# Streaming output projection in another chunk order, an indexer without GpSimd, and a solve and an input that come in pieces

## The chip, the cores and the metric

The kernel runs on one core of a Trainium2 chip. The metric is the device time of one execution in microseconds (us). The engines are TensorE (PE in the rows, with its weight loads as PEld), VectorE (DVE), ScalarE (ACT), GpSimd (POOL) and SyncE (SP, which here only issues DMAs); 16 DMA engines serve the core's queues.

## What is computed

One layer of an encoder block on x of 256 tokens by 2048 channels, in fp32. One input projection feeds two groups of heads: sparse attention (8 heads x 128, with an indexer that keeps each query's 64 highest-scored admissible keys) and RWKV-7 time mixing (16 heads x 64). Their outputs, side by side, go through one output projection; then comes a mixture of 16 experts.

```python
h = rms_norm(x, g_mix)
proj = h @ w_in
y_dsa = dsa_mixer(...)             # indexer scores, top-k, softmax attention
y_rwkv = rwkv7_mixer(...)          # token shift, delta-rule scan, group norm, gate
x = x + concat(y_dsa, y_rwkv) @ w_out
h = rms_norm(x, g_ffn)
# hier_moe: 1 of 4 groups, 2 of its 4 experts per token, SwiGLU experts
x = x + hier_moe(h, ...)
```

## The kernel before

**Weights stream.** Both projections are matmuls in which each fp32 weight is used as the sum of two fp32r parts, and so is the input (three products each). `drive()` walks one long list, `stream`, of chunks of 128 partitions x 512 columns of weights: SP loads two at a time (512 KB) into three raw places (`RA` lower and upper half, `RB`), up to 8 chunks ahead; ACT copies a chunk to its high part (line 205), DVE subtracts it from the raw chunk to get the low part (line 206), into four slots `W`; PE then runs that chunk's matmuls (`pp`). `add_cm` chunks belong to RWKV's input blocks (12 matmuls of 256 columns), `add_tm` chunks to attention's columns and to the output projection (6 matmuls of 512 columns: 3 products for each of 2 token halves). A column chunk c0 to c3 of the output projection is 512 output columns and 16 chunks of the stream, one for each 128 channels of the mixed output: r0 to r7 from the RWKV blocks, h0 to h7 from the attention heads. `YSLOTS` gives their order in each column chunk, and a chunk needs the event that its `y` is there. Two banks `pp` hold a column chunk's sums, of four.

**What sets the order.** PE's order is written out by a planner, `Order`, that keeps its own time: generators (chains) yield a number (come back so much later) or a name (come back after that event), and between two chunks of the stream `drive()` lets every chain run that is ready. The chains are `rwkv_early(b)`, `solve(b)` and `rwkv_late(b)` for the 8 RWKV blocks (128 channels each), `kidx`, `qidx`, `qk`, `indexer` and `attention` for the sparse attention, `spread` for the input's norm, and `u_chain(cc)` behind each column chunk. The other engines' order is made by a scheduler from the program's order and the waits.

**RWKV blocks.** `rwkv_early(b)` ends with small matrices written to DRAM (`din`). `solve(b)` is on POOL: it reads `din` back, each partition its own copy (`at`, 512 KB in one DMA, line 650), then does 31 steps of a triangular solve on `xt` (two tensor_tensor each, lines 655 and 657; step s reads column s of `at`), and sends the result out and back (`dout`, `XT`: lines 658 and 660). `rwkv_late(b)` starts on PE with the matmul `pz<-R,XT`, then `pz<-z,A`, `pq`, `pc`, `pS`, `py`, `ptp`, `pv`, and gives chunk `r{b}` (`yT`).

**Attention.** `indexer()` builds scores `acc` on DVE query block by query block; a POOL memset masks a corner of it (line 872), then 8 rounds of `max` and `match_replace` on DVE find the top 64. Each head's `yps` and `ptp` matmuls give h0 to h7.

**The input's norm.** x (2 MB) is loaded in one DMA (`xt_`) behind the first weights; ACT squares it in four pieces with sums, `rstd` follows, and `spread()` makes `rsB` (1/rms for all tokens on every partition) by one matmul `rps` after a fixed 16.1 us. The first use of `rsB` is `shift()`, which frees a block's `pp` bank; DSA's columns use `rstd`.

**Behind the mixers.** When c0 is summed, `u_done(0)` calls `enter_moe()`: it asks for the event "rw closed" (the last `rwkv_late` is over) and all y, sets up the MoE's tiles, and POOL loads x again by column chunk (`load_x(cc)`, to `uu`; x(0) there, the others from within the output projection, line 1168, each behind a POOL copy that waits for the newest `W`). `u_chain(cc)` adds the sums to `uu`, transposes it (`utp`, 8 matmuls, copied to `uT`) and makes the router's logits `pl`; c(n) needs `u(n-1)` before its own `u_chain`.

**Expert weights.** 192 chunks of 1 MB go through a ring of 20 places, some of which are the space of `hT`, `W`, `RA` and others that must first be free. The first three are loaded after the last `rwkv_early`; `leave_rwkv` loads the next after the last `rwkv_late`, `prefetch_step` then one for every 2.2 weight loads, and at step c = 3 of c3 a burst fills the ring up to `n_early` = 15 chunks (line 1171), with one more each at c = 3, 7, 11 and 15. All are SP DMAs, in SP's order with the loads of `wo`. The experts' phase then runs pair after pair.

Of the kernel before, what the change touches and what calls it, by code (L numbers as in the profile page):

```python
# [17 lines left out]
P = 128  # L18
T = 256
D = 2048  # L20
# [7 lines left out]
CLAMP = -80.0  # L28

CON = [("cent", P), ("mask_s", 64), ("mask_bd", P), ("mask21", 64), ("scanm", T), ("xt0", 128), ("mu", 27), ("vecs", 64)]  # L30
YSLOTS = ["r0", "r1", "r2", "r3", "r4", "r5", "h0", "h1", "h2", "h3", "r6", "r7", "h4", "h5", "h6", "h7"]
EB1, EB2, EB = 9, 4, 20
FIRST = 1
WARM = 19
# [82 lines left out]
def block_kernel(ctx: ExitStack, tc: tile.TileContext, a: dict, dbg=None):  # L117
# [121 lines left out]
    with tc.tile_pool(name="xload", bufs=1) as xp:  # L239
        gT = xp.tile([P, KT], F32, name="gT")  # L240
        SP.dma_start(out=gT, in_=a["gT"])
        xT = [xp.tile([P, 4, T], F32, name=f"xT{q}") for q in range(4)]
        xt_ = xp.tile([P, 2, D], F32, name="xt_")

        def load_xT(q, r0, r1):
            SP.dma_start(out=xT[q][:, r0:r1, :], in_=a["xT"][:, 4 * q + r0:4 * q + r1, :])

        def load_w(n):
            c = (0, 1, 0)[n] * 1024
            return load_raw(a["wr"][(1, 1, 0)[n], :, c:c + 1024], 2 if n == 0 else 1)  # L250

        load_xT(0, 0, 2)
        raw0 = load_w(0)
        load_xT(0, 2, 4)
        load_xT(1, 0, 4)
        raw1 = load_w(1)
        load_xT(2, 0, 4)
        load_xT(3, 0, 4)
        first[0].update(zip((4, 5), load_w(2)))
        SP.dma_start(out=ident, in_=a["ident"])  # L260
        SP.dma_start(out=xt_, in_=a["x"].rearrange("(j p) m -> p j m", p=P))
        for q in range(4):
            for r in range(4):
                if q == 0 and r == 1:
                    first[1].update({k: split(raw0[k]) for k in range(2)})
                if q == 1 and r == 2:
                    first[1].update({2 + k: split(raw1[k]) for k in range(2)})
                g = gT[:, 4 * q + r:4 * q + r + 1]
                hi = hT[q][:, 0, r, :]
                ACT.activation(out=hi, in_=xT[q][:, r, :], func=AF.Copy, scale=g)  # L270
                DVE.scalar_tensor_tensor(out=hT[q][:, 1, r, :], in0=xT[q][:, r, :], scalar=g, in1=hi.bitcast(F32), op0=ALU.mult, op1=ALU.subtract)
        sq = xp.tile([P, D // 2], F32, name="sq")
        part = xp.tile([P, 2, 2], F32, name="part")
        for j in range(2):
            for c in range(2):
                ACT.activation(out=sq, in_=xt_[:, j, c * (D // 2):(c + 1) * (D // 2)], func=AF.Square, accum_out=part[:, j, c:c + 1])
        DVE.tensor_tensor(out=rstd, in0=part[:, :, 0], in1=part[:, :, 1], op=ALU.add)
        ACT.activation(out=rstd, in_=rstd, func=AF.Ln, scale=1.0 / D, bias=eps6)
        ACT.activation(out=rstd, in_=rstd, func=AF.Exp, scale=-0.5)

    def spread():

        yield RSTD_US
        ps = pbank("rps")
        dg = temp("kd")
        for j in range(2):
            DVE.tensor_scalar(dg[:, j * P:(j + 1) * P], ident, rstd[:, j:j + 1], None, ALU.mult)
        mm(ps[:, 0:T], ones, dg)
        ACT.copy(out=rsB, in_=ps[:, 0:T])
        od.event("rsB", Y[22])  # L290
# [29 lines left out]
    def tables():  # L320
        cs128 = att.tile([P, 2, 2, 64], F32, name="cs128", tag="qr", bufs=2)
        gq = att.tile([P, 2, 128], F32, name="gq", tag="qo", bufs=2)
        SP.dma_start(out=cs128, in_=a["cs128"])
        SP.dma_start(out=cs64, in_=a["cs64"])
        SP.dma_start(out=gq[:, 0, :], in_=a["q_gain"].broadcast_to([P, 128]))
        SP.dma_start(out=gq[:, 1, :], in_=a["k_gain"].broadcast_to([P, 128]))
        for s in range(2):
            for j in range(2):
                for hf in range(2):
                    g1 = gq[:, s, hf * 64:(hf + 1) * 64]  # L330
                    go = gq[:, s, (1 - hf) * 64:(2 - hf) * 64]
                    POOL.tensor_tensor(out=cg[:, s, j, hf * 64:(hf + 1) * 64], in0=cs128[:, j, 0, :], in1=g1, op=ALU.mult)
                    POOL.tensor_tensor(out=sg_[:, s, j, hf * 64:(hf + 1) * 64], in0=cs128[:, j, 1, :], in1=go, op=ALU.mult)
                POOL.tensor_scalar(sg_[:, s, j, 0:64], sg_[:, s, j, 0:64], -1.0, None, ALU.mult)
        POOL.tensor_scalar(sn64[:, :, 0, :], cs64[:, :, 1, :], -1.0, None, ALU.mult)
        POOL.tensor_copy(sn64[:, :, 1, :], cs64[:, :, 1, :])
# [189 lines left out]
    def rwkv_early(b):  # L526
# [15 lines left out]
        cs = temp("e1")  # L542
        DVE.tensor_tensor_scan(cs, scanm, sa[:, 0, :], 0.0, ALU.mult, ALU.add)
        Dt = temp("Dt", 2)[:, 0:260].rearrange("p (c t) -> p c t", c=4)
        POOL.memset(Dt[:, :, 0:1], 1.0)
        ACT.activation(out=Dt[:, :, 1:65], in_=cs.rearrange("p (c t) -> p c t", c=4), func=AF.Exp, scale=-C0)
        di = temp("di")
        ACT.activation(out=di, in_=cs, func=AF.Exp, scale=C0)
# [95 lines left out]

    def solve(b):

        at = tmp.tile([P, 32, 32], F32, name="at", bufs=1)
        xt = tmp.tile([P, 4, 32], F32, name="xt", bufs=1)
        tt = tmp.tile([P, 128], F32, name="tt", bufs=1)
        SQ.dma_start(out=at, in_=dr[b][0].rearrange("(o ci) u s t -> o (ci u) (s t)", o=1).broadcast_to([8, 16, 1024]))  # L650
        POOL.tensor_copy(xt, xt0)
        for s_ in range(31):
            n, m = s_ // 8 + 1, 31 - s_
            tv = tt[:, 0:n * m].rearrange("p (u t) -> p u t", u=n)
            POOL.tensor_tensor(out=tv, in0=xt[:, 0:n, s_:s_ + 1].broadcast_to([P, n, m]),  # L655
                               in1=at[:, s_:s_ + 1, s_ + 1:32].broadcast_to([P, n, m]), op=ALU.mult)
            POOL.tensor_tensor(out=xt[:, 0:n, s_ + 1:32], in0=xt[:, 0:n, s_ + 1:32], in1=tv, op=ALU.subtract)  # L657
        SQ.dma_start(out=dr[b][1].rearrange("ci w (i q) t -> q (ci w) i t", q=8), in_=xt.rearrange("p i t -> p (i t)"))
        for ci in range(4):
# [187 lines left out]
    def indexer():  # L847
# [3 lines left out]
        for j in range(2):  # L851
# [3 lines left out]
            for q in range(4):  # L855
# [13 lines left out]
                        else:  # L869
                            DVE.scalar_tensor_tensor(out=acc[:, :nk], in0=rl[:, b2, :nk], scalar=wx[:, j, hd:hd + 1], in1=acc[:, :nk], op0=ALU.mult, op1=ALU.add)  # L870
                yield 2 * Y[17]
            POOL.memset(acc[0:64, nk - 64:nk], NEG)
            for _ in range(8):
                m8 = att.tile([P, 8], F32, name="m8", bufs=2)
                DVE.max(m8, acc[:, :nk])
# [137 lines left out]
    def enter_moe():  # L1013
# [20 lines left out]
        xv = a["x"].rearrange("(j p) m -> p j m", p=P)  # L1034
        mo_["xv"] = xv
        load_x(0)
        for n in ("wrt", "gF", "iota", "utri", "rsum"):
            POOL.dma_start(out=mo_[n], in_=a[n])
        POOL.tensor_tensor(out=mo_["wrt"], in0=mo_["wrt"], in1=mo_["gF"].rearrange("p (k o) -> p k o", o=1).broadcast_to([P, KT, 32]), op=ALU.mult)
# [126 lines left out]

    def wo_after(cc):
        def after(c):
            if c == 4 and cc:
                load_x(cc)  # L1170
            if c % 4 == 3 and cc == 3:
                while len(ring) < n_early:
                    load_chunk(len(ring), True)
                load_chunk(len(ring) + 1)
        return after

    for cc in range(4):
# [354 lines left out]
```

## Times and profile before

| | |
|---|---|
| median of 3 runs | 1102.25 us (1102.21 to 1104.61) |
| the profiled execution | 1108.09 us |
| its span, first to last instruction | 1106.1 us |
| PE busy | 1034.8 us (94%) |
| DVE, ACT, POOL busy | 535.7, 384.0, 258.6 us |
| mean granted TensorE clock | 0.973 |
| moved by DMA | 298.74 MB, mean 270 GB/s |

The profile is one execution. Its span leaves 1.99 us of that execution's 1108.09 us to what lies around it. In the rows, an idle time in brackets stands before the first of a group of instructions on that engine, with what released it. A granted clock of 0.50 is the lower of TensorE's two levels, 1.2 of 2.4 GHz.

### The profile page before, as it was taken

What the parts mean: (1) busy time and instruction counts of PE and PEld (TensorE: products, weight loads), DVE (VectorE), ACT (ScalarE), POOL (GpSimd) and SP (SyncE); (2) the same over time, 40 slices, a digit from 0 to 9 for tenths busy, and PEclk for the clock granted to TensorE, in tenths of its full rate; (3) what the DMA queues carried; (4) which work ended last, traced back from release to release, by engine and by line L of the source; (5) the groups of instructions that cost most, each with busy time, mean ns of one, the idle gap of its engine ahead of it and who ended that gap; (6) DMA issues with size and microseconds to landing.
All of it is one profiled execution on the core that took longest, in us unless ns stands there. A gap on an engine that the chain in (4) does not pass through costs nothing.

```text
span 1106.1 us, 17189 instructions
## 1 busy us (share of the span) xinstructions
PE 1034.8 (94%) x6466; PEld 698.7 (63%) x6466; DVE 535.7 (48%) x1193; ACT 384.0 (35%) x816; POOL 258.6 (23%) x666
## 2 busy tenths in 40 slices
PE   5999999989899999898799789999999999999996
PEld 5999888967698877686577654444444343434342
DVE  5887668777768776855354231313121313121212
ACT  6666555646446564644244211000000101010101
POOL 1416572648346535353110100000000000000000
PEclk9999999999999998998799899999999999999998
DMA  8566554454345543445299969999999999999995
GB/s 317 166 187 191 162 153 150 124 140 127 118 141 181 161 143 101 141 124 207 72 331 330 394 252 364 364 420 420 420 421 421 420 420 419 421 420 420 420 417 202
DMA packets 62266, 298.74 MB, mean 270 GB/s; under 512 B 9040, under 2 KB 12928, under 8 KB 37856
## 3 DMA queue, kind: packets, MB, share of 16 engines
q1 hardware_dynamic: 56720, 289.29, 69.6%
q0 software_dynamic: 5456, 8.28, 3.1%
q8 instruction: 53, 0.87, 0.3%
q14 instruction: 37, 0.30, 0.1%
HBM read 294.37 MB, written 3.15 MB: 269 GB/s over the span
## 4 chain that ended last, share of the span: by engine, by line
PE 77%; DMA 7%; DVE 5%; ACT 4%; POOL 3%; issue 2%; SPq 1%; ACTq 0%; DVEq 0%; POOLq 0%
PE pp L130 27%; PE pd L130 10%; PE gate L130 10%; PE up L130 10%; PE misc L130 6%; DMA RA<-wo 4%; PE sc L130 3%; PE pz L130 2%; DVE W L206 2%; PE py L130 2%; DMA xt__114<-x 1%; POOL xt L657 1%; ACT W L205 1%; POOL tt L655 1%; PE pc L130 1%
## 5 line engine op out<-in xcount | busy, mean ns | idle before, releaser
L130 PE MATMUL pp<-W,hT 128*128 128x512 f32 x768 | 194.3, 405 | 6.5 <-DVE W L206 6.5
L206 DVE TENSOR_TENSOR W<-RA,W 128x512 fp32r<-128x512 f32 x200 | 137.5, 697 | 98.9 <-ACT W L205 97.0
L130 PE MATMUL pp<-hT,W 128*128 128x256 f32 x1296 | 174.0, 292 | 11.8 <-ACT W L205 10.5
L130 PEld LDWEIGHTS pp<-hT,W 128*128 128x128 f32 x1296 | 164.5, 197 | 15.7 <-ACT W L205 10.7
L205 ACT CAST W<-RA 128x512 fp32r<-128x512 f32 x200 | 122.1, 619 | 133.5 <-PE pp L130 87.6
L130 PEld LDWEIGHTS pp<-W,hT 128*128 128x128 f32 x768 | 144.4, 193 | 38.0 <-DVE W L206 7.4
L130 PE MATMUL pp<-W,yT 128*128 128x512 f32 x384 | 99.5, 414 | 13.7 <-ACT yT L890 6.6
L655 POOL TENSOR_TENSOR tt<-xt,at 128x24 f32<-128x24 f32 (+23 forms) x248 | 89.6, 361 | 72.8 <-DMA at<-din 54.1
L130 PEld LDWEIGHTS pp<-W,yT 128*128 128x128 f32 x384 | 74.4, 198 | 34.0 <-ACT W L205 8.0
L657 POOL TENSOR_TENSOR xt<-xt,tt 128x24 f32<-128x24 f32 (+23 forms) x248 | 89.1, 359 | 19.3
L206 DVE TENSOR_TENSOR W<-RB,W 128x512 fp32r<-128x512 f32 x100 | 68.7, 695 | 38.8 <-ACT W L205 38.3
L130 PE MATMUL pd<-ew,R 128*64 128x512 f32 x352 | 81.1, 598 | 2.7 <-ACT R L1376 2.7
L205 ACT CAST W<-RB 128x512 fp32r<-128x512 f32 x100 | 61.0, 619 | 60.4 <-PE pp L130 45.5
L130 PE MATMUL up<-ew,R 128*64 128x512 f32 x352 | 79.3, 592 | 0.0
L130 PEld LDWEIGHTS misc<-sel,uu 128*128 128x128 f32 x512 | 59.6, 192 | 15.2 <-issue 13.8
L1386 ACT ACTIVATE Y<-pd,sv 128x512 fp32r<-128x512 f32 x32 | 22.0, 688 | 126.8 <-PE pd L130 126.8
L1387 DVE SCALAR_TENSOR_TENSOR Y<-pd,sv,Y 128x512 fp32r<-128x512 f32 x32 | 24.0, 751 | 83.0 <-ACT Y L1386 83.0
L130 PE MATMUL misc<-sel,uu 128*128 128x128 f32 x512 | 63.0, 278 | 0.7 <-DVE sel L1308 0.7
L1396 DVE TENSOR_TENSOR x<-x,sc 128x512 f32<-128x512 f32 x56 | 36.0, 685 | 54.9 <-PE sc L130 54.9
L130 PE MATMUL gate<-ew,R 128*64 128x512 f32 x272 | 61.7, 595 | 0.0
L1318 DVE TENSOR_TENSOR R<-misc,gF 128x512 f32<-128x512 f32 x28 | 19.4, 691 | 79.5 <-PE misc L130 79.5
L130 PEld LDWEIGHTS up<-ew,R 128*64 128x64 f32 x352 | 25.3, 137 | 50.2 <-issue 49.4
(371 smaller groups left out, 1217.2 us busy)
## 6 DMA issues: line engine op xcount, KB each, us to landing
ew<-we SPq DMA_DIRECT2D x91, 1024.0 KB, 19.1
ew<-wdn SPq DMA_DIRECT2D x40, 1024.0 KB, 17.7
ewh<-we SPq DMA_DIRECT2D x24, 1024.0 KB, 17.4
RA<-wd SPq DMA_DIRECT2D x43, 512.0 KB, 3.6
RA<-wr SPq DMA_DIRECT2D x35, 512.0 KB, 4.0
ewh<-wdn SPq DMA_DIRECT2D x12, 1024.0 KB, 19.8
RB<-wd SPq DMA_DIRECT2D x21, 512.0 KB, 3.6
RA<-wo SPq DMA_DIRECT2D x21, 512.0 KB, 6.3
```

The lines of the kernel that those rows point to most:

```text
L130: PE.matmul(out, lhsT=lhsT, rhs=rhs, start=start, stop=stop, skip_group_check=skip)
L205: ACT.copy(out=hi, in_=raw)
L206: DVE.tensor_tensor(out=lo, in0=raw, in1=hi.bitcast(F32), op=ALU.subtract)
L655: POOL.tensor_tensor(out=tv, in0=xt[:, 0:n, s_:s_ + 1].broadcast_to([P, n, m]), in1=at[:, s_:s_ + 1, s_ + 1:32].broadcast_to([P, n, m]), o ...
L657: POOL.tensor_tensor(out=xt[:, 0:n, s_ + 1:32], in0=xt[:, 0:n, s_ + 1:32], in1=tv, op=ALU.subtract)
L1318: DVE.tensor_tensor(out=t, in0=ps.rearrange("p (a t) -> p a t", t=P), in1=gF[:, 4 * kq:4 * kq + 4].rearrange("p (a o) -> p a o", o=1).broa ...
L1386: ACT.activation(out=yh, in_=pd, func=AF.Copy, scale=sv[:, 1:2])
L1387: DVE.scalar_tensor_tensor(out=yl, in0=pd, scalar=sv[:, 1:2], in1=yh.bitcast(F32), op0=ALU.mult, op1=ALU.subtract)
L1396: DVE.tensor_tensor(out=x1[j][:, ns], in0=(uu[:, j, ns] if first else x1[j][:, ns]), in1=ps, op=ALU.add)
```

## The change

In the output projection r7 moves to the last slot of each column chunk, and c0 and c1 are taken in turn: ten chunks of c0, ten of c1, the last six of c0, the last six of c1; then c2 and c3 as before. `xt_` is gone: x comes in four DMAs of 512 KB into `yr` and `qT`, the squares, `rstd` and `dg` are issued from `spread()` 8.0 us of the planner's time after the start and piece by piece, `rps` later, and a block's `done` now asks for the event "rsB". The tables' four DMAs go from SP's queue to POOL's. `Dt`'s memset is issued for block 0 only. The solve's matrix comes in two tiles by two DMAs, columns 0 to 7 (128 KB) and 8 to 31 (384 KB). The memset in the indexer goes from POOL to DVE. x(1) is loaded right behind x(0), and the ring's burst is issued at c = 7 of c3, with two chunks at 7 and one each at 11 and 15 behind it.

```diff
-YSLOTS = ["r0", "r1", "r2", "r3", "r4", "r5", "h0", "h1", "h2", "h3", "r6", "r7", "h4", "h5", "h6", "h7"]
+YSLOTS = ["r0", "r1", "r2", "r3", "r4", "r5", "h0", "h1", "h2", "h3", "r6", "h4", "h5", "h6", "h7", "r7"]
+AHEAD = 10
...
-        SP.dma_start(out=xt_, in_=a["x"].rearrange("(j p) m -> p j m", p=P))
...
-        sq = xp.tile([P, D // 2], F32, name="sq")
-        part = xp.tile([P, 2, 2], F32, name="part")
+
+    def spread():
+
+        yield 8.0
+        part = const.tile([P, 2, 2], F32, name="part")
+        xv = a["x"].rearrange("(j p) (c m) -> p j c m", p=P, c=2)
+        xs = [t.rearrange("p b t -> p (b t)").rearrange("p (c m) -> p c m", c=2) for t in (yr, qT)]
         for j in range(2):
             for c in range(2):
-                ACT.activation(out=sq, in_=xt_[:, j, c * (D // 2):(c + 1) * (D // 2)], func=AF.Square, accum_out=part[:, j, c:c + 1])
+                SP.dma_start(out=xs[j][:, c, :], in_=xv[:, j, c, :])
+                yield 1.0
+        for j in range(2):
+            for c in range(2):
+                ACT.activation(out=vt[:, j, :], in_=xs[j][:, c, :], func=AF.Square, accum_out=part[:, j, c:c + 1])
+                yield 1.0
...
-    def spread():
-
-        yield RSTD_US
-        ps = pbank("rps")
         dg = temp("kd")
         for j in range(2):
             DVE.tensor_scalar(dg[:, j * P:(j + 1) * P], ident, rstd[:, j:j + 1], None, ALU.mult)
+        yield 3.0
+        ps = pbank("rps")
         mm(ps[:, 0:T], ones, dg)
...
+                od.need(["rsB"])
                 t = temp(nm)
                 st[b][nm] = t
                 shift(ps, 3 + 3 * b + n, t)
...
-        at = tmp.tile([P, 32, 32], F32, name="at", bufs=1)
+        at = [tmp.tile([P, n, 32], F32, name=f"at{n}", bufs=1) for n in (8, 24)]
...
-        SQ.dma_start(out=at, in_=dr[b][0].rearrange("(o ci) u s t -> o (ci u) (s t)", o=1).broadcast_to([8, 16, 1024]))
+        for t, r0, r1 in ((at[0], 0, 8), (at[1], 8, 32)):
+            SQ.dma_start(out=t, in_=dr[b][0][:, :, r0:r1, :].rearrange("(o ci) u s t -> o (ci u) (s t)", o=1).broadcast_to([8, 16, 32 * (r1 - r0)]))
...
-            POOL.memset(acc[0:64, nk - 64:nk], NEG)
+            DVE.memset(acc[0:64, nk - 64:nk], NEG)
...
         load_x(0)
+        load_x(1)
...
-            if c == 4 and cc:
+            if c == 4 and cc > 1:
                 load_x(cc)
-            if c % 4 == 3 and cc == 3:
+            if c == 7 and cc == 3:
                 while len(ring) < n_early:
                     load_chunk(len(ring), True)
+            if c % 4 == 3 and c > 3 and cc == 3:
                 load_chunk(len(ring) + 1)
+                if c == 7:
+                    load_chunk(len(ring) + 1)
...
+    c0, c1 = stream[-64:-48], stream[-48:-32]
+    stream[-64:-32] = c0[:AHEAD] + c1[:AHEAD] + c0[AHEAD:] + c1[AHEAD:]
```

What POOL has in a row where one solve ends and the next begins while the indexer works, before (`acc` are the scores, `din` and `dout` the solve's matrices in DRAM; `G` is a place in which `Dt` lies):

```order
L658 DMA dout_213<-xt 8x64x32
L660 DMA XT_197<-dout_213 32x4x32 x4
L651 COPY xt<-con 128x128
L545 MEMSET G_89 128x4
L872 MEMSET acc 64x64
L606 DMA din_214<-AB 32x4x32 x4
L650 DMA at<-din_214 128x1x1024
L655 TENSOR_TENSOR tt<-xt,at 128x31
```

And now:

```order
L667 DMA dout_202<-xt 8x64x32
L669 DMA XT_186<-dout_202 32x4x32 x4
L660 COPY xt<-con 128x128
L614 DMA din_203<-AB 32x4x32 x4
L659 DMA at_2852<-din_203 128x1x256
L659 DMA at_2853<-din_203 128x1x768
L664 TENSOR_TENSOR tt<-xt,at_2852 128x31
```

Both memsets have left POOL, and the DMA of the matrix is two. On PE, the end of the attention and of the last RWKV block (`pp` are chunks of the stream, 6 matmuls each; `yps` and `ptp` belong to attention, `pz`, `pq` and `pv` to the RWKV blocks), before:

```order
L140 MATMUL ptp<-ident,L 128x128 x3
L130 MATMUL pv<-y__5909,bones_r 128x256 x2
L130 MATMUL pp<-W_84,yT_5580 128x512 x6
L140 MATMUL ptp<-ident,L 128x128 x3
L130 MATMUL pz_5971<-R,XT_198 128x128 x4
...
L130 MATMUL pz_5997<-z_5969,A_5967 64x128 x8
L130 MATMUL pz_6007<-R,XT_198 128x128 x4
L130 MATMUL pq<-MM,WG 64x128 x4
```

And now:

```order
L131 MATMUL pp<-W_83,yT_5407 128x512 x6
L131 MATMUL pp<-W_84,yT_5590 128x512 x12
L131 MATMUL pp<-W_83,yT_5590 128x512 x6
L131 MATMUL pz_6065<-R,XT_187 128x128 x4
L131 MATMUL yps<-PT,vt 128x256
...
L131 MATMUL pp<-W_83,yT_5590 128x512 x6
L131 MATMUL pz_6100<-z_6063,A_6061 64x128 x8
L131 MATMUL pp<-W_84,yT_5675 128x512 x12
L131 MATMUL pz_6127<-R,XT_187 128x128 x4
L131 MATMUL pp<-W_83,yT_5675 128x512 x6
L131 MATMUL pq<-MM,WG 64x128 x4
```

Thirteen chunks of the stream stand between the `py` of the block before the last and the last block's `pq`, where one stood. Behind `pq` there is no chunk until the last block's `pv`, before and now. On PE, from that `pv` on, before:

```order
L130 MATMUL pv<-y__6074,bones_r 128x256 x2
L130 MATMUL pp<-W_84,yT_5580 128x512 x6
L130 MATMUL pp<-W_83,yT_5696 128x512 x12
...
L130 MATMUL pp<-W_84,yT_5399 128x512 x12
L140 MATMUL utp<-ident,uu 128x128 x4
L130 MATMUL pp<-W_83,yT_5580 128x512 x12
L140 MATMUL utp<-ident,uu 128x128 x4
```

And now:

```order
L131 MATMUL pv<-y__6205,bones_r 128x256 x2
L131 MATMUL pp<-W_83,yT_5675 128x512 x6
L131 MATMUL pp<-W_84,yT_5590 128x512 x12
L131 MATMUL pp<-W_83,yT_5675 128x512 x12
L131 MATMUL pp<-W_84,yT_5675 128x512 x12
L141 MATMUL utp<-ident,uu 128x128 x8
L131 MATMUL pl<-uT,wrt 32x256 x4
L131 MATMUL pp<-W_83,yT_5358 128x512 x12
```

Seven chunks are left of c0 and c1 behind the last block, and c0's transposes and logits stand between them and c2, with no chunk among them.

## Rows read from the trace of the kernel before

**Rows 1.** The span in stretches: up to the first squares, the mixers, the end of the mixers, the output projection behind them, the change-over, the experts. Columns: stretch, its us, then busy us (and instructions) of PE, PEld, DVE, ACT, POOL, the granted TensorE clock, the DMA engines' busy share, GB/s.

```profile
24.60:515.00 490.40, 466.11 (x3526) 404.13 (x3527) 359.93 (x833) 281.61 (x618) 242.72 (x619) 0.97 0.50 150
515.00:546.70 31.70, 20.95 (x180) 16.18 (x178) 12.63 (x37) 11.09 (x30) 0.86 (x3) 0.79 0.19 69
546.70:650.50 103.80, 93.43 (x450) 72.99 (x450) 44.06 (x102) 38.90 (x79) 13.09 (x33) 0.95 0.90 335
650.50:708.00 57.50, 56.77 (x296) 25.64 (x298) 12.15 (x23) 5.04 (x8) 0.00 (x0) 1.00 0.87 329
708.00:1085.00 377.00, 371.39 (x1894) 163.29 (x1890) 87.79 (x162) 29.36 (x47) 0.00 (x0) 1.00 1.01 418
```

**Rows 2.** The first 40 us in order of time, all engines. Columns: start, us, engine, line, operation, out<-in, count, and in brackets the idle time before it and what released it.

```profile
20.05 1.06 ACT L276 ACTIVATE sq<-xt__114 128x1024 f32<-128x1024 f32 x1 [3.26 <-DMA xt__114<-x]
23.94 1.12 ACT L205 CAST W<-RA 128x512 fp32r<-128x512 f32 x2
24.59 10.59 PE L130 MATMUL pp<-hT,W 128*128 128x256 f32 x72 [4.64 <-ACT W L205]
35.02 0.59 PE L130 MATMUL rps<-G 128*128 128x256 f32 x2
36.36 0.42 DVE L415 TENSOR_TENSOR G<-pp,rsB 128x256 f32<-128x256 f32 x1
```

**Rows 3.** Stretches in which the granted clock was 0.50, with the columns of rows 1.

```profile
24.66:28.07 3.41, 3.41 (x15) 3.16 (x16) 2.78 (x6) 3.31 (x8) 1.67 (x3) 0.50 0.72 247
130.47:133.88 3.41, 3.41 (x19) 3.41 (x18) 0.00 (x0) 0.60 (x2) 0.63 (x1) 0.50 0.58 201
236.28:239.69 3.41, 3.41 (x14) 2.55 (x13) 3.34 (x13) 1.76 (x5) 2.17 (x4) 0.50 0.14 24
290.89:294.30 3.41, 3.41 (x10) 2.63 (x9) 3.41 (x10) 0.62 (x1) 0.00 (x0) 0.50 0.45 137
502.52:505.94 3.42, 3.42 (x21) 2.79 (x18) 0.88 (x4) 1.17 (x7) 2.64 (x13) 0.50 0.00 0
523.00:526.41 3.41, 3.41 (x12) 2.72 (x12) 0.42 (x2) 0.93 (x2) 0.00 (x0) 0.50 0.02 5
```

**Rows 4.** Groups of DMA issues. Columns: out<-in, queue, count, KB each, median us from issue to landing.

```profile
at<-din POOLq DMA_DIRECT2D x8, 512.0 KB, 7.3
uu<-x POOLq DMA_DIRECT2D x4, 512.0 KB, 7.9
dout<-xt POOLq DMA_DIRECT2D x8, 64.0 KB, 3.9
wrt<-wrt POOLq DMA_DIRECT2D x1, 256.0 KB, 5.1
```

**Rows 5.** PE in order of time, the waits between 120 and 505 us in which a late block, the indexer and the end of the attention take part (columns as in rows 2).

```profile
129.91 1.32 PE L130 MATMUL pz<-R,XT 128*128 128x128 f32 x7 [2.49 <-DMA XT<-dout]
...
236.03 1.37 PE L130 MATMUL ips<-kiT,qiT 64*128 64x256 f32 x5 [3.76 <-DVE MM L601]
...
290.54 1.79 PE L130 MATMUL pp<-W,hT 128*128 128x512 f32 x4 [4.37 <-DVE W L206]
...
415.29 0.46 PE L130 MATMUL lps<-kT,qT 128*128 128x128 f32 x2 [2.16 <-DVE MM L601]
...
471.05 0.89 PE L130 MATMUL yps<-PT,vt 128*128 128x256 f32 x4 [2.12 <-DVE MM L601]
...
500.88 0.66 PE L130 MATMUL pq<-MM,WG 128*64 128x128 f32 x8 [1.68 <-DVE sm L908]
```

**Rows 6.** DVE in order of time, at the indexer's first `max` of a query block.

```profile
234.65 0.29 DVE L875 MAX8 m<-acc 128x8 f32<-128x128 f32 x1 [4.95 <-POOL acc L872]
...
289.47 0.43 DVE L875 MAX8 m<-acc 128x8 f32<-128x256 f32 x1 [6.86 <-POOL acc L872]
```

**Rows 7.** PE in order of time, 515 to 570 us: the end of the last RWKV block.

```profile
522.72 2.71 PE L130 MATMUL pp<-W,yT 128*128 128x512 f32 x6 [3.38 <-ACT yT L890]
...
531.62 1.16 PE L130 MATMUL pz<-R,XT 128*128 128x128 f32 x8 [0.79 <-DVE R L687]
533.45 0.66 PE L130 MATMUL pq<-MM,WG 128*64 128x128 f32 x8 [0.68 <-ACT WG L692]
...
542.40 1.04 PE L130 MATMUL pv<-y__6074,bones_r 128*128 128x256 f32 x2 [0.98 <-ACT y__6074 L473]
546.71 19.67 PE L130 MATMUL pp<-W,yT 128*128 128x512 f32 x78 [3.27 <-ACT yT L890]
```

**Rows 8.** SP's issues, ACT and PE, 609 to 629 us, in order of time: the end of the output projection.

```profile
613.66 0.93 SPq L1092 DMA_DIRECT2D ew<-we  x2
...
614.70 0.36 SPq L193 DMA_DIRECT2D RA<-wo  x1
...
627.89 1.14 ACT L205 CAST W<-RA 128x512 fp32r<-128x512 f32 x2 [7.00 <-DMA RA<-wo]
...
628.56 0.80 PE L130 MATMUL pp<-W,yT 128*128 128x512 f32 x1 [5.55 <-ACT W L205]
```

**Rows 9.** POOL and ACT in order of time behind the last RWKV block: a memset, x(0)'s load and the first copy to `uT`.

```profile
546.36 0.20 POOL L1033 MEMSET ones<- 128x128 f32 x1 [30.70 <-DVE yr L759]
...
548.70 0.73 POOL L1011 DMA_DIRECT2D uu<-x  x1
...
567.55 0.58 ACT L1140 COPY uT<-utp 128x512 f32<-128x512 f32 x1
```

More of the change, by code (lines that the diff above doesn't have):

```diff
@@ L242, in block_kernel @@
         xT = [xp.tile([P, 4, T], F32, name=f"xT{q}") for q in range(4)]
-        xt_ = xp.tile([P, 2, D], F32, name="xt_")
         def load_xT(q, r0, r1):
@@ L322, in tables @@
         gq = att.tile([P, 2, 128], F32, name="gq", tag="qo", bufs=2)
[L323 to L326, printed above, removed]
+        POOL.dma_start(out=cs128, in_=a["cs128"])
+        POOL.dma_start(out=cs64, in_=a["cs64"])
+        POOL.dma_start(out=gq[:, 0, :], in_=a["q_gain"].broadcast_to([P, 128]))
+        POOL.dma_start(out=gq[:, 1, :], in_=a["k_gain"].broadcast_to([P, 128]))
         for s in range(2):
@@ L544, in rwkv_early @@
         Dt = temp("Dt", 2)[:, 0:260].rearrange("p (c t) -> p c t", c=4)
-        POOL.memset(Dt[:, :, 0:1], 1.0)
+        if b == 0:
+            POOL.memset(Dt[:, :, 0:1], 1.0)
         ACT.activation(out=Dt[:, :, 1:65], in_=cs.rearrange("p (c t) -> p c t", c=4), func=AF.Exp, scale=-C0)
@@ L655, in solve @@
             POOL.tensor_tensor(out=tv, in0=xt[:, 0:n, s_:s_ + 1].broadcast_to([P, n, m]),
-                               in1=at[:, s_:s_ + 1, s_ + 1:32].broadcast_to([P, n, m]), op=ALU.mult)
+                               in1=at[s_ >= 8][:, s_ % 8 if s_ < 8 else s_ - 8, s_ + 1:32].rearrange("p (o t) -> p o t", o=1).broadcast_to([P, n, m]), op=ALU.mult)
             POOL.tensor_tensor(out=xt[:, 0:n, s_ + 1:32], in0=xt[:, 0:n, s_ + 1:32], in1=tv, op=ALU.subtract)
```

## The prediction

> **What bounds the kernel now.** I read the table of stretches first [rows 1]. From 24.6 to 515 us the mixers run: PE is busy 466.11 of 490.40 us, DVE 359.93, the DMA engines half of the time. So PE's work is the bound, and what can be won is PE's idle time (24.3 us there), and the time lost to the lower clock (0.97 on the mean). From 515 to 546.7 PE is busy only 20.95 of 31.70 us at a clock of 0.79: the last RWKV block ends alone. Then the output projection has 10.4 us of idle in 103.8. From 708 to 1085 the DMA engines are full (1.01, 418 GB/s) and PE is busy 371.39 of 377: both at their limit, and this change does nothing to that stretch but start it sooner. So I added up PE's waits ahead of 650 us, looked at who releases each, and at the stretches of clock 0.50 that stand behind several of them [rows 3]: in 3.41 us at half clock 1.7 us are lost. A second list is what the DMAs cost that these waits hang on [rows 4].
>
> **The change part by part.** The sum is made against the profiled span, 1106.1 us. That execution took 1108.09 us, 5.8 us above the median of 1102.25; I take the saving off the median.
>
> *Start.* PE waits 4.64 us at 24.59 for ACT's copy of W at 23.94, which stands behind ACT's four squares of x, and these waited 3.26 us for the 2 MB load [rows 2]; 3.41 us at half clock follow [rows 3]. The squares now wait for pieces and stand behind the streams' copies, so this goes: 4.64 + 1.7 = 6.3 us. Against it, `rps` stands behind the fourth block's matmuls, and the fifth block needs a bank that only `shift()` frees: matmul, copy and multiply took from 35.02 to 36.78 us, 1.8 us [rows 2], and this can lower the clock once more (1.7 us). Ends 1 and 4.5, **I take 3.0**. Of the x load itself nothing is saved, since the 2 MB are the same. The tables' four DMAs leave SP and stand on POOL ahead of the first solve; POOL waits for `din` there anyway, so 0.
>
> *Solve.* The first late block waited 2.49 us for XT [rows 5], with 3.41 us at half clock behind it [rows 3]: 4.2 us. Its chain now has the 128 KB piece in place of the 512 KB one. That piece has no row; the nearest are 3.9 us for 64 KB and 5.1 us for 256 KB, so it saves between 2.2 and 3.4 of 7.3 us [rows 4], and the remaining 24 columns are needed only eight steps later. Ends 1.5 and 4.2, **4.0 taken**. The seven other solves get shorter too, but their late blocks did not wait.
>
> A rule speaks against this term: the Trainium skill, "DMA: Bandwidth & Descriptors", section "Anatomy of one DMA — SWDGE (gpsimd) path", gives such a transfer a fixed 2.0 us and then 436 GB/s; my estimate by it is 2.3 us for 128 KB and 3.2 us for 512 KB, so that 1.6 us of the wait would stay, and the total would be about 1073 us. The trace does not agree with it: the 512 KB transfer took 7.3 us [rows 4].
>
> *Indexer.* DVE stood 4.95 and 6.86 us at the first `max` of a query block, because the memset waits in POOL's order behind the end of a solve [rows 6]; the splits of W and the `MM` masks queue behind that `max`, and PE waited 3.76 us for MM and 4.37 us for W [rows 5], with half clock behind each [rows 3]. On DVE the memset waits for nothing. 3.76 + 4.37 + 2 x 1.7 = 11.5 us. DVE gets the memsets themselves: a larger one took 0.20 us on POOL [rows 9], and four times that would still be under 2 us for all. What may be late next is DVE's own work, 73% busy here [rows 1]. Ends 7 and 11.5, **10.5 taken**.
>
> *Other waits of the mixers.* Those at 415.29 and 471.05 (2.16 and 2.12 us) [rows 5] have DVE as releaser and none of the parts as cause; earlier blocks and another order shift them, to better or worse. Ends -4 and +10, **2 taken**, nearest to one of them gone.
>
> *End of the last block.* Twelve more chunks of the stream are now between the block before the last and the last one's `pv`. They need no result of that block, so they fill PE's waits at 500.88 (1.68) [rows 5], 522.72 (3.38), 531.62 (0.79) and 533.45 (0.68) [rows 7], and the two stretches of half clock at 502 and 523 us [rows 3], 3.4 us: 9.9 us together. From `pq` to r7's chunk, 533.45 to 546.71, PE stays bare as before: the 0.98 and 3.27 us [rows 7] and the half clock there remain. Ends 5 and 11, **9.5 taken**.
>
> *Behind it.* Before, c0's transposes stood among chunks of c1 that were there to run. Now six chunks of c1 are all that is left, about 9 us (13 chunks took 19.67 us, 1.5 each [rows 7]), then c2 stands behind c0's sums, which wait for x(0): 7.9 us from an issue that came 2 us after r7 [rows 4, 9]. Then two uu additions, 8 `utp`, the copies to `uT` (0.58 us each [rows 9]) and `pl` stand bare. A new wait: ends 0.5 and 6, **-2.5 taken**. x(1) being sooner costs nothing; it is covered by c2.
>
> *End of the output projection.* The burst's expert loads on SP stand ahead of a load of `wo` to RA at 614.70 us, which ACT got only at 627.89, and PE waited 5.55 us [rows 8], with some us of half clock behind it, here estimated as one stretch of rows 3. With the burst behind the last `wo` load this goes: ends 2 and 7.4, **6 taken**. Cover for the burst itself is the router's stretch, where the DMA engines were 0.87 busy [rows 1].
>
> Sum: 3.0 + 4.0 + 10.5 + 2 + 9.5 - 2.5 + 6 = 32.5 us; 1102.25 - 32.5 = **1070 us** (span about 1074).
> The terms' ends, taken as independent, lie 10 us to the one side and 9 to the other: 1061 to 1080 for the forecast alone.
>
> **The rivals.**
>
> *The expert weights don't follow.* The ring opens at the end of the last block. Before, 12 of the stream's 64 chunks of `wo` were done by then and 52 left, now 26 and 38; with loads 8 chunks ahead that is 22 pairs of loads to pace the ring by, now 15, one expert chunk per 2.2 pairs: 10 and 7. Three chunks of 1 MB less until the burst, 3.1 MB or 7.5 us at 418 GB/s [rows 1], and the burst four chunks (6 us) later: if the router's stretch doesn't take that up, and the last weights decide, 13 us are given back: 1083. For it: 418 GB/s up to 1085 us, no reserve there. Against it: 0.87 and 329 GB/s from 650.5 to 708 [rows 1] leave 5 MB of room.
>
> *The waits come back elsewhere.* PE's order is fixed by the planner; four new waits like those at 415 and 471 us [rows 5], each with 1.7 us of half clock, cost 4 x 3.8 = 15 us: 1085. For it: DVE's 73%. Against it: in 490 us of mixers all idle time of PE was 24.3 us [rows 1].
>
> *Slower: the last block is pushed back.* The twelve chunks stand ahead of its end, 18 us of PE. If the waits they should fill are those of the block's own chain through DVE and ACT, and each chunk's split (two of ACT's copies took 1.12 us [rows 2]) stands in that chain too, it gets 12 x 0.56 = 6.7 us longer, and with the low ends of the first three terms (9.5 us) the ring opens 18 + 6.7 - 9.5 = 15.2 us later than at 546.7. It has 3.1 MB less of `wo` to share with (7.5 us), and the burst is 6 us later: 13.7 us, 1116 us, if the last weights decide. It decides from a ring that opens 1.5 us later than before, 548 us. By my terms it opens at 546.7 + 18 - 17.5 - 9.5 = 537.7.
>
> *The change doesn't do it:* the waits at 236 and 290 us are put down to the memset, but the semaphore that came last could be another, and the filled waits be replaced by the new ones: 1102.
>
> **How the numbers follow.** Forecast 0.57, weights 0.18, waits elsewhere 0.15, pushed back 0.05, nothing 0.05. The likeliest is the forecast, 1070. The range takes in the forecast's own and the two middle rivals with a few us around, and leaves out the two last and the forecast's thinnest edge: 1058 to 1088. This kernel can be told from no change from 0.3% on, 3.3 us. Faster by more than that: 0.57 + 0.18 + 0.15, that is 0.90; within it 0.05, slower 0.05.
>
> **What would show it.** Right: no ACT wait for x at 20 us and PE's first longer wait only at `rps`; no wait of DVE on POOL at line 881; no 2.49 us before the first late block's `pz`; 515 to 547 us without a wait over 1 us before `pq`, and the ring's first paced load near 538; a wait of some 2 us on PE at `utp` before c2; no wait of 5 us near the end of the output projection; the experts' stretch as before, some 32 us sooner, at 418 GB/s. Wrong: PE waits for `ew` at the experts' start or end (the weights), a clock of 0.50 at new places among the mixers (waits elsewhere), a ring that opens after 548 us (pushed back), a wait of over 6 us at `utp`.

## The result, and the profile after

The changed kernel takes 1074.01 us (median of 4 runs, 1070.9 to 1077.22) against 1102.26; the ratio is 0.9739, 95% interval 0.9707 to 0.977. That is 28.25 us; 32.5 were forecast. The profiled execution took 1077.22 us, span 1075.2; its mean granted clock is 0.989 (0.973 before). Each of the two profiled executions is longer than every other run of its kernel in that comparison.

The stretches after, cut at the places that answer to [rows 1] (mixers, end of the mixers, output projection, change-over, experts; columns as there):

```profile
24.60:494.00 469.40, 452.80 (x3522) 392.89 (x3520) 357.64 (x832) 284.31 (x623) 241.91 (x611) 1.00 0.54 160
494.00:535.80 41.80, 36.22 (x269) 29.14 (x265) 22.53 (x53) 19.68 (x45) 2.59 (x6) 0.97 0.44 143
535.80:619.00 83.20, 74.58 (x366) 58.33 (x366) 35.25 (x88) 30.95 (x65) 13.56 (x33) 0.93 0.95 354
619.00:677.00 58.00, 57.21 (x298) 25.80 (x300) 12.21 (x24) 5.48 (x8) 0.00 (x0) 1.00 0.91 357
677.00:1054.00 377.00, 371.40 (x1894) 163.33 (x1892) 88.23 (x163) 28.93 (x47) 0.00 (x0) 1.00 1.01 418
```

The experts take the same 377 us with the same 418 GB/s: what was won lies ahead of 619 us. In the mixers the clock is 1.00, not 0.97; the waits of 2.49, 3.76 and 4.37 us of [rows 5] and of 4.95 and 6.86 us on DVE [rows 6] have gone, and so have the half-clock stretches behind them [rows 3]. Of the two waits at 415.29 and 471.05 us [rows 5] the first has gone, and the second stands now at 453.86 us and is longer:

```profile
453.86 0.92 PE L131 MATMUL yps<-PT,vt 128*128 128x256 f32 x4 [2.96 <-DVE yT L900]
```

The groups of DMA issues of the solve, which answer to [rows 4]:

```profile
at<-din POOLq DMA_DIRECT2D x8, 384.0 KB, 6.5
...
at<-din POOLq DMA_DIRECT2D x8, 128.0 KB, 3.4
dout<-xt POOLq DMA_DIRECT2D x8, 64.0 KB, 4.7
```

The 128 KB piece lands in 3.4 us where 512 KB took 7.3; the forecast was 3.9 to 5.1. PE at the start, in order of time, with the waits that answer to [rows 2]:

```profile
13.30 16.73 PE L131 MATMUL pp<-hT,W 128*128 128x256 f32 x114 [4.79 <-ACT hT L269]
...
31.43 0.50 PE L131 MATMUL pp<-hT,W 128*128 128x256 f32 x2 [1.40 <-ACT W L206]
...
36.04 0.50 PE L131 MATMUL pp<-hT,W 128*128 128x256 f32 x2 [0.98 <-ACT W L206]
...
44.18 7.45 PE L131 MATMUL pp<-hT,W 128*128 128x256 f32 x60 [1.21 <-DVE G L421]
...
59.23 2.89 PE L131 MATMUL pp<-hT,W 128*128 128x256 f32 x22 [1.39 <-DVE W L207]
```

The 4.64 us at 24.59 have gone, and 4.79 stand at 13.30, with four of 0.98 to 1.40 us behind it: the waits of the start have moved, and have not become shorter. On ACT, at that time:

```profile
12.15 0.62 ACT L206 CAST W<-RA 128x512 fp32r<-128x512 f32 x1 [5.64 <-DMA RA<-wr]
```

Before, ACT began this copy, the second piece of weights, at 6.33 us after a wait of 0.54 us. The end of the last block on PE, answering to [rows 7]:

```profile
531.66 0.84 PE L131 MATMUL pv<-y__6205,bones_r 128*128 128x256 f32 x2 [0.98 <-ACT y__6205 L479]
535.77 11.84 PE L131 MATMUL pp<-W,yT 128*128 128x512 f32 x42 [3.27 <-ACT yT L899]
547.45 1.03 PE L141 MATMUL utp<-ident,uu 128*128 128x128 f32 x8
549.69 0.64 PE L131 MATMUL pl<-uT,wrt 128*32 128x256 f32 x8 [1.21 <-issue]
```

The 3.38, 0.79 and 0.68 us are filled; 0.98 and 3.27 stay, as forecast. `utp` waits for nothing, so x(0) was there; only 1.21 us stand before `pl`, for which the profile names no releaser. r7's chunk starts at 535.77 (546.71 before), with fourteen more chunks done.

### The profile page after: what moved, and what is told of

It reads as the page before. It is cut to its first block, busy times and chain, and to the rows that moved or that the text cites. A ratio compares the mean times of both kernels' runs of the same rounds, so it can differ in the third digit from the quotient of the medians.

```text
span 1075.2 us, 17230 instructions
## 1 busy us (share of the span) xinstructions
PE 1017.9 (95%) x6466; PEld 686.1 (64%) x6466; DVE 535.5 (50%) x1195; ACT 385.2 (36%) x816; POOL 264.8 (25%) x669
## 4 chain that ended last, share of the span: by engine, by line
PE 70%; DVE 5%; DMA 3%; ACT 2%; issue 2%; POOL 0%; SPq 0%; DVEq 0%; ACTq 0%
PE pp L131 21%; PE pd L131 11%; PE gate L131 10%; PE up L131 10%; PE misc L131 6%; PE sc L131 3%; DMA RA<-wo 3%; PE pz L131 2%; PE py L131 2%; DVE W L207 1%; ACT W L206 1%; PE pc L131 1%; PE lps L131 1%; PE misc L141 1%; PE tps L141 0%
## 5 line engine op out<-in xcount | busy, mean ns | idle before, releaser
L131 PE MATMUL pp<-W,hT 128*128 128x512 f32 x768 | 189.5, 398 | 1.6 <-DVE W L207 1.6
L131 PE MATMUL pp<-hT,W 128*128 128x256 f32 x1296 | 171.2, 289 | 16.9 <-ACT W L206 8.9
L131 PEld LDWEIGHTS pp<-hT,W 128*128 128x128 f32 x1296 | 161.5, 194 | 21.3 <-ACT W L206 9.4
L131 PEld LDWEIGHTS pp<-W,hT 128*128 128x128 f32 x768 | 141.1, 189 | 31.9 <-DVE W L207 2.0
L664 POOL TENSOR_TENSOR tt<-xt,at 128x24 f32<-128x24 f32 (+23 forms) x248 | 86.7, 349 | 37.8 <-DMA at<-din 19.0
L1345 ACT CAST selT<-misc 128x256 fp32r<-128x256 f32 x8 | 3.0, 372 | 154.5 <-PE misc L131 154.5
```

Source lines behind the costliest of these rows:

```text
L131: PE.matmul(out, lhsT=lhsT, rhs=rhs, start=start, stop=stop, skip_group_check=skip)
L1345: ACT.copy(out=selT, in_=ps[:, 0:T])
```

## The experiments

Each is timed beside the kernel before on the same chip; that kernel's medians were 1100.5 us (beside runs 1, 2, 3 and 7), 1099.82 (4, 9, 11 and the base) and 1099.98 (5, 6, 8, 10). Differences between kernels below are of medians; the changed kernel itself has 1072.67 us (ratio 0.9758, 0.9737 to 0.978), which serves as base:

> The changed kernel as it is, beside the other kernels of this call, on their chip. Every theory: a ratio of 0.974 to the kernel before, within 0.003, about 1072 us where the kernel before takes 1100.5.

**1. The tables' DMAs back on SP.**

```diff
-        POOL.dma_start(out=cs128, in_=a["cs128"])
+        SP.dma_start(out=cs128, in_=a["cs128"])
```
(and the three lines behind it alike)

> The changed kernel with the four DMAs of the tables back on SP's queue (in SP's order they stand behind the first weights). Theory: on POOL's queue they are issued at 1.9 to 3.1 us, and while they are served the weights and x^T, issued at the same time on SP, land 6 us later than before (a load of 256 KB issued at 2.14 us landed at 12.13, before at 6.31), so PE waits 4.79 us at 13.3 us. Back on SP that wait goes: 1074 - 4 = about 1070 us, and the first weights land by 6.5 us. Rival: the start is bound by the bytes that must come before the first 35 us are over (x too), whichever queue carries the tables: the wait at 13.3 us moves to the next loads and the time stays within 1.5 us of 1074.

1074.05 us (ratio 0.9769, 0.9747 to 0.979), 1.4 us more than the base, with intervals that overlap: no difference is shown. PE at the start:

```profile
9.34 17.14 PE L131 MATMUL pp<-hT,W 128*128 128x256 f32 x114 [1.55 <-ACT hT L269]
...
30.22 11.75 PE L131 MATMUL pp<-hT,W 128*128 128x256 f32 x72 [3.74 <-ACT W L206]
```

The wait at 13.3 us shrinks to 1.55 and one of 3.74 us comes at 30.22, where ACT's copy of W stands behind its squares of x. The tables do hold the weights back, but the theory that this costs 4 us falls. The rival fits: the wait moved and the time stayed. That the bytes of the first 35 us are the reason is argued; no run loads fewer.

**2. The memset back on POOL.**

```diff
-            DVE.memset(acc[0:64, nk - 64:nk], NEG)
+            POOL.memset(acc[0:64, nk - 64:nk], NEG)
```

> The changed kernel with the indexer's memset back on POOL. Theory (the prediction's term of 10.5 us; between the marks around the two places the trace after is 11.3 us ahead): DVE waits for POOL at the first max of two query blocks again, and the time is 9 to 12 us longer, about 1084. Rival: with the solves shortened by the split of their matrix, POOL reaches the memsets earlier, and most of the wait is gone without the move: 0 to 4 us longer.

1072.0 us (0.975, 0.973 to 0.9771): no difference at all, though the trace of the changed kernel had won 11 us around these two places. My theory falls, and the rival (0 to 4 us longer) holds. DVE's one wait for that memset that is left:

```profile
274.36 0.43 DVE L884 MAX8 m<-acc 128x8 f32<-128x256 f32 x1 [0.56 <-POOL acc L881]
```

**3. The solve's matrix in one tile and one DMA.**

```diff
-        at = [tmp.tile([P, n, 32], F32, name=f"at{n}", bufs=1) for n in (8, 24)]
+        at = tmp.tile([P, 32, 32], F32, name="at", bufs=1)
```
(with the one DMA and the one index of the kernel before)

> The changed kernel with the solve's matrix in one tile and one DMA of 512 KB. Theory (the prediction's term of 4.0 us): only the first late block waits for a solve; PE waits about 2.5 us before its pz and loses 1.7 us to the clock: 4 us longer, about 1078. Rival: the later start of the first block gives the solve time, the wait does not come back: within 1 us. A second rival: the seven other solves count too, since each late block stands nearer to its solve now: more than 7 us longer.

1079.51 us (0.9838, 0.9807 to 0.9869), 6.8 us longer: above the theory's 4 and just under the second rival's 7. The first late block does not wait; a later one does, which none of the waits of [rows 5] was:

```profile
290.59 1.81 PE L131 MATMUL pz<-R,XT 128*128 128x128 f32 x8 [2.21 <-DMA XT<-dout]
```

So the second rival's mechanism holds: the other solves count.

**4. Both undone.** The edits of 2 and 3 together.

> The changed kernel with both undone: the memset on POOL and the solve's matrix in one tile. Alone the first cost nothing and the second about 7 us. Theory: the two stand in for each other; POOL came late to the memset because its chain of solves was late, so with whole solves the memset is late again and DVE waits for it at both places: 3 to 8 us more than the 7 us, about 1084. Rival: the memset never mattered in this order of the stream, and PE's wait there is for XT alone: the same time as with the matrix in one tile alone, within 1.5 us.

1089.08 us (0.9912, 0.988 to 0.9945), 16.4 us longer. DVE waits for POOL as in [rows 6]:

```profile
235.03 0.29 DVE L883 MAX8 m<-acc 128x8 f32<-128x128 f32 x1 [4.72 <-POOL acc L880]
...
285.70 0.43 DVE L883 MAX8 m<-acc 128x8 f32<-128x256 f32 x1 [7.79 <-POOL acc L880]
```

The theory's mechanism holds; its size was too small: 9.6 us more than run 3, where 3 to 8 were expected, with runs that spread from 1085.02 to 1096.16. POOL's chain of solves shows why. Run 2 and this run differ in the pieces alone. Here POOL waits long for `at`, sends the solve out at 279.15 us and reaches the second memset at 285.49:

```profile
250.55 0.23 POOL L663 TENSOR_TENSOR tt<-xt,at 128x31 f32<-128x31 f32 x1 [9.39 <-DMA at<-din]
...
279.15 1.01 POOL L666 DMA_DIRECT2D dout<-xt  x1 [0.30 <-POOL xt L665]
...
285.49 0.17 POOL L880 MEMSET acc<- 64x64 f32 x1
```

In run 2, the same three steps:

```profile
238.61 0.76 POOL L664 TENSOR_TENSOR tt<-xt,at 128x31 f32<-128x31 f32 x1 [2.11 <-DMA at<-din]
...
266.67 1.02 POOL L667 DMA_DIRECT2D dout<-xt  x1 [0.30 <-POOL xt L666]
...
274.16 0.17 POOL L881 MEMSET acc<- 64x64 f32 x1
```

There POOL is 11.3 to 12.5 us further: the pieces bring it to the memset in time, and then it is worth nothing to take the memset off POOL.

**5 and 6. One of them alone in the kernel before.** The same edits, forwards.

> The kernel before with the solve's matrix in two pieces and nothing else. Theory: POOL's chain of solves is what both waits of the indexer's memset hang on, about 3 us late more with each solve; with the pieces POOL is there in time, so this alone brings most of the 16 us that the changed kernel loses when both edits are undone: 10 to 16 us shorter than before, about 1086, with no wait of DVE on POOL at the first max. Rival (the prediction's terms): only the first late block's wait goes, 4 us shorter.

> The kernel before with the indexer's memset on DVE and nothing else. Theory: DVE's waits of 4.95 and 6.86 us at the first max go, but the late block behind the second now stands before its solve: 6 to 9 us shorter, about 1092. Rival (the prediction's term): 10.5 us shorter, 1089. Second rival: XT, late by the same chain, takes the whole of the wait over: under 3 us shorter.

The pieces alone: 1089.1 us, 10.9 us shorter than the kernel before (0.9906, 0.9876 to 0.9936). The memset alone: 1096.08 us, 3.9 us shorter (0.9964, 0.9938 to 0.999). The first bears the theory out (10 to 16). The second lies between the theory (6 to 9) and the second rival (under 3), and its interval of 1.1 to 6.8 us touches both. In its profile DVE no longer waits for POOL at the `max`, the first late block still waits for XT, and at the end of the output projection PE waits somewhat longer than in [rows 8]:

```profile
131.21 1.13 PE L130 MATMUL pz<-R,XT 128*128 128x128 f32 x8 [2.60 <-DMA XT<-dout]
...
615.08 7.07 PE L130 MATMUL pp<-W,yT 128*128 128x512 f32 x18 [6.46 <-ACT W L205]
```

That profiled execution is 9.1 us shorter than the one of before (1098.95 and 1108.09), the medians only 3.9 apart, with runs from 1093.08 to 1103.53; what makes that spread stays open. With the pieces alone the first late block's `pz` does not wait, and DVE's two waits at the first `max` are almost gone, with the memset still on POOL:

```profile
227.26 0.29 DVE L876 MAX8 m<-acc 128x8 f32<-128x128 f32 x1 [1.23 <-POOL acc L873]
...
274.14 0.43 DVE L876 MAX8 m<-acc 128x8 f32<-128x256 f32 x1 [0.27 <-POOL acc L873]
```

**7. The order of the chunks as before.** `YSLOTS` of before, and c0 to c3 one after the other (`AHEAD = 16`).

> The changed kernel with the slots of before (r7 twelfth) and the four column chunks one after the other. Theory: the terms on the end of the last block and behind it (9.5 - 2.5) are lost, 6 to 10 us longer, about 1082, with waits before the last block's pz and pq as before. Rival: what the trace shows as won there was won by the earlier solve and the memset (the block's chain comes sooner), and the new order gives it back at the transposes before c2: 0 to 3 us longer.

1079.51 us (0.9822, 0.9801 to 0.9843), 6.8 us longer: the theory (6 to 10).

**8. r7 last, but one column chunk after the other.**

```diff
-AHEAD = 10
+AHEAD = 16
```

> The changed kernel with r7 in the last slot, but c0 to c3 one after the other. Theory: c0's four chunks h4 to h7, now ahead of r7, fill the waits for attention and part of the last block's chain, and the interleaving gives the other nine chunks and takes the bare transposes before c2; of the 7 us that the old order costs, most comes with the slot alone: 0 to 3 us longer than the changed kernel. Rival (the prediction's sum, 9.5 - 2.5 by twelve chunks): four chunks fill too little, 4 to 7 us longer.

1079.63 us (0.9814, 0.978 to 0.9848), 7.0 us longer, as much as in run 7, where the slot too is as before. The rival holds: the slot alone brings nothing, and the chunks of c1 are needed to fill the waits. The interleaving with r7 in its old slot was not run. The first of [rows 7] is back to its old size:

```profile
500.87 2.59 PE L131 MATMUL pp<-W,yT 128*128 128x512 f32 x6 [3.38 <-ACT yT L899]
```

**9. The start of before.** x in one load, its squares in the setup, `rps` after 16.1 us of the planner's time, tables on SP.

```diff
-            ACT.activation(out=vt[:, j, :], in_=xs[j][:, c, :], func=AF.Square, accum_out=part[:, j, c:c + 1])
+            ACT.activation(out=sq, in_=xt_[:, j, c * (D // 2):(c + 1) * (D // 2)], func=AF.Square, accum_out=part[:, j, c:c + 1])
...
-        yield 8.0
+        yield RSTD_US
```

> The changed kernel with the start of before: x in one load behind the first weights, its squares in the setup, rps after 16.1 us of the planner's time, tables on SP. Theory: the new start gains nothing; up to the end of the fourth block PE was 0.8 us later than before in the profile after, since the bytes that ACT waits for are the same and only the place of the wait moved, and the new wait behind rps takes the rest: the same time, within 2 us of the changed kernel, with the 4.6 us wait at 24 us back. Rival (the prediction's term): 3 us longer, up to 4.5.

1076.51 us (0.9788, 0.9769 to 0.9807), 3.8 us longer: the rival's number, so my theory falls, but not by the rival's mechanism. The first 70 us with the start of before:

```profile
0.00:70.00 70.00, 57.23 (x415) 55.35 (x416) 51.32 (x117) 46.13 (x97) 14.30 (x37) 0.95 0.65 231
```

and of the changed kernel beside it:

```profile
0.00:70.00 70.00, 55.12 (x416) 52.80 (x417) 49.92 (x111) 45.23 (x94) 16.52 (x41) 1.00 0.67 230
```

PE has 415 and 416 matmuls behind it at 70 us: what the new start has more in waits the old one has in half clock. Further on the old start is ahead: the same `pS` of an RWKV block comes at 372.34 us with it and at 375.80 in the changed kernel. Then, up to another block's `pS`, it loses 7.0 us. With the start of before:

```profile
372.34 0.33 PE L131 MATMUL pS<-S,Ph 64*64 64x64 f32 x4
...
423.31 0.33 PE L131 MATMUL pS<-S,Ph 64*64 64x64 f32 x4
```

In the changed kernel:

```profile
375.80 0.33 PE L131 MATMUL pS<-S,Ph 64*64 64x64 f32 x4
...
419.78 0.33 PE L131 MATMUL pS<-S,Ph 64*64 64x64 f32 x4
```

The 3.8 us are what is left of both. Between those marks, with the start of before, PE stands here:

```profile
400.79 0.46 PE L131 MATMUL lps<-kT,qT 128*128 128x128 f32 x2 [2.16 <-DVE MM L604]
401.71 0.67 PE L131 MATMUL lps<-kT,qT 128*128 128x256 f32 x2 [0.47 <-DVE MM L604]
404.09 0.90 PE L141 MATMUL ptp<-ident,L 128*128 128x128 f32 x3 [1.71 <-DVE R L691]
```

The first of them is the wait of 2.16 us at 415.29 in [rows 5], to the hundredth. It stands in all four kernels with the start of before (the kernel before and runs 5, 6 and 9), and in no trace with the new one. In the changed kernel `lps` and `ptp` stand ahead of the masks `pa` there:

```profile
398.54 0.81 PE L131 MATMUL lps<-kT,qT 128*128 128x128 f32 x4
399.19 0.49 PE L141 MATMUL ptp<-ident,L 128*128 128x128 f32 x3
399.61 1.26 PE L131 MATMUL pa<-G 64*64 64x128 f32 x29
```

That the planner's clock, moved by the other start, put them so, is argued from the two orders; no run moved that clock alone.

**10. The ring's burst at c = 3 as before.**

```diff
-            if c == 7 and cc == 3:
+            if c == 3 and cc == 3:
```
(and one chunk each at 3, 7, 11 and 15)

> The changed kernel with the ring's burst at c = 3 of c3 as before, and one chunk each at 3, 7, 11 and 15. Theory: PE waits longer at the end of the output projection (5.55 us before, 1 to 3.5 in the changed kernel), 2 to 4 us longer, about 1075.5. Rival (the prediction's term): 6 us longer. Second rival: the four chunks' time doesn't change what stands ahead of the last loads of wo: within 1 us.

1086.85 us (0.9889, 0.9857 to 0.992), 14.2 us longer: more than any of the three expected. PE waits at the end of the output projection, and SP's issues say for what:

```profile
603.39 7.46 PE L131 MATMUL pp<-W,yT 128*128 128x512 f32 x18 [13.95 <-ACT W L206]
```

```profile
577.64 0.33 SPq L1102 DMA_DIRECT2D ewh<-wdn  x1
579.02 0.93 SPq L1102 DMA_DIRECT2D ewx<-we  x2
580.00 3.11 SPq L1102 DMA_DIRECT2D ew<-we  x4
583.21 0.44 SPq L194 DMA_DIRECT2D RA<-wo  x1
584.97 0.33 SPq L194 DMA_DIRECT2D RB<-wo  x1
```

Seven expert chunks, 7.3 MB or 17.6 us at 418 GB/s, stand ahead of the last two loads of `wo`. In the kernel before the wait was 5.55 us [rows 8], with three expert chunks ahead of the last two loads (at 611.20 and 613.66 us on SP): the new order of the chunks leaves fewer loads to pace the ring by, so more of it comes in the burst, and the burst's later place is what the new order needs.

**11. Every load of `wo` ahead of the burst.** Paced expert loads stop after the 12th pair, the burst comes at c = 11, its hoisted loads gated.

```diff
+        pairs[0] += room > 0
+        if pairs[0] > HOLD:
+            return
...
-            if c == 7 and cc == 3:
+            if c == 11 and cc == 3:
...
-                load_chunk(len(ring) + 1)
+                load_chunk(len(ring) + 1, True)
```

> The changed kernel with the end of the output projection's loads put apart: no paced expert load after the 12th pair, the burst at c = 11 of c3, with its hoisted loads gated too, so that every load of wo stands ahead of the burst on SP. Theory: the 1 to 3.5 us for which PE waits near the end of the projection, and the spread of 6 us between runs of the changed kernel, come from two or three expert loads ahead of the last loads of wo: the wait goes, 1 to 3 us shorter than the changed kernel. Rival: the DMA engines are full there, and expert weights that come later are waited for at the start of the experts or at the end of the span: the same time or up to 6 us longer.

1070.17 us (0.973, 0.971 to 0.975), 2.5 us shorter than the changed kernel; the runs lie at 1068.5 to 1072.12 against 1071.49 to 1075.9. The wait there is gone; on PE between 540 and 605 us only these are left:

```profile
549.97 0.64 PE L132 MATMUL pl<-uT,wrt 128*32 128x256 f32 x8 [0.85 <-issue]
...
600.48 0.64 PE L132 MATMUL pl<-uT,wrt 128*32 128x256 f32 x8 [1.18 <-ACT uT L1155]
601.61 0.62 PE L132 MATMUL pv<-rsum,lgT 128*128 128x20 f32 x4 [0.49 <-ACT lgT L1166]
```

The expert weights, later in part, were not waited for: behind 630 us PE's longest wait is 0.9 us, as in the base. This is the fastest of all the kernels here; the intervals of the two ratios overlap by 0.0013, so it is likely, not certain.

`Dt`'s memset and the earlier load of x(1) were not undone in any run.

## Why the prediction was right, and where its steps were not

The time (1074.01 of 1070 forecast, within 1058 to 1088) and the sign came out, and the forecast was its likeliest case. Term by term it was less good, and some errors cancelled.

*Solve (4.0) and indexer (10.5).* Together 14.5 were forecast and 16.4 measured. The split between them was wrong. The step that failed: "The seven other solves get shorter too, but their late blocks did not wait." They form one chain on POOL, and the memset stood in it; shortening the chain took the memset's wait away too. In the kernel before, the pieces alone are worth 10.9 us and the memset alone 3.9. In the changed kernel the pieces put last are worth 6.8 us and the memset put last nothing; without the pieces the memset is worth 9.6 (runs 3 and 4), near the forecast's 10.5. So the memset's price hangs on what else is changed; why it is 3.9 in the one kernel with whole solves and 9.6 in the other stays open. The pieces' price left out what they do to POOL's chain: the first three waits of [rows 5] and the two of [rows 6] were read one by one, with one edit each, and run 5 shows that the pieces alone take them all, but for 1.23 us. The small transfer took 3.4 us, less than the 3.9 to 5.1 taken for it.

The Trainium skill, "DMA: Bandwidth & Descriptors", section "Anatomy of one DMA — SWDGE (gpsimd) path", gives a fixed 2.0 us and 436 GB/s; the estimate by it was 2.3 and 3.2 us for the two sizes, by which the piece would be worth 0.9 us. The measurement decides against it here: 3.4 us for 128 KB, and 7.7 us for the 512 KB of run 3, so it was worth 4.3. What makes these transfers dearer than the rule no run shows.

*Start (3.0).* By the traces even its sign was wrong. The step that failed is that the wait "goes": the squares' 4.64 us went, and the weights and x, whose bytes are the same, were waited for at other places. By one trace each of run 9 and of the base the start of before is 3.5 us ahead at 372 us; the 3.8 us that its undoing costs come from elsewhere (the next term). The tables' move at "0" agrees with the time of run 1, but its reason, POOL's wait for `din`, missed the mechanism: the move held the first weights back, and in run 1 as much was waited for behind x.

*Other waits (2, ends -4 and +10).* Taken was "nearest to one of them gone", and one is gone, that at 415.29 us; run 9's trace loses 7.0 us where it comes back. The other is longer (2.96 us). The prediction gave no cause by which one should go, so that this came out is luck; its range was honest. It is also luck that this gain covers what the start lost: the two terms together, 5.0 in the forecast, are the 3.8 us of run 9.

*End of the last block and behind it (9.5 - 2.5).* 7.0 forecast, 6.8 measured by run 7 and 7.0 by run 8, filled by the chunks of c1 as forecast; `utp` did not wait, and `pl` 1.21 us.

*End of the output projection (6).* Mis-sized: in the profiles of the changed kernel and of runs 1 and 2 PE still waits 0.83 to 3.47 us there, of 5.55, and run 11 gets 2.5 us more. In run 7, with the chunks in the order of before and the burst in its new place, PE does not wait there, so the wait that is left comes with the new order. In exchange the burst's later place prevents 14.2 us that the new order would have cost: the rival of the expert weights had counted that order's bunching rightly (three chunks fewer paced), only not where it bites, ahead of the last loads of `wo`.

*The slower rival* was refuted by its own mark: r7's chunk, with which the ring opens, starts at 535.77 us, near the 537.7 forecast, and not after 548.

The single undoings add up to more than was won (16.4 + 6.8 + 3.8 + 14.2 = 41 of 27.2 us beside the base): edits that need each other, the burst and the order, are counted twice. Without the burst they come to 27.0.

## What to carry to other kernels

When several waits are released by one engine, look at that engine's own chain before giving each its price: one shortening can take them all, and an edit beside it that looks necessary may be worth nothing. A change of order that removes slots from a paced prefetch makes the rest of that prefetch a burst; look at what stands behind it in the queue. A wait for bytes can move when the order of loads changes, without becoming shorter: compare the same instruction further on in both traces before a wait that has gone is counted as won.

## What was not expected of the hardware

Three loads from POOL's queue at 1.9 to 3.1 us (128 KB and twice 64 KB) held back loads of SP's queue issued at the same time. In the nine traces with these loads on POOL's queue ACT's copy of the second piece of weights begins at 8.27 to 12.15 us, in the five with them in SP's order at 6.33 to 7.74; in run 1, which differs from the changed kernel in this alone, at 7.03 us:

```profile
7.03 0.62 ACT L206 CAST W<-RA 128x512 fp32r<-128x512 f32 x1 [1.24 <-DMA RA<-wr]
```

So it is some 1 to 5 us, and not the same in each execution. The wait of PE at that place is 4.79 us in the changed kernel's first trace, 4.05 in the base's and 1.55 in run 1.

Kernels with the solve in one piece spread more from run to run (1077.81 to 1088.25 in run 3, 1085.02 to 1096.16 in run 4) than the same with pieces (1071.49 to 1075.9 for the base, 1071.24 to 1073.39 in run 2); why is open.
